# Two-layer hybrid encoder: matmuls grouped by shape, one pool of PSUM slots, three pieces of elementwise work on GpSimd

## The chip, the cores and the metric

The kernel runs on one core of a Trainium2 chip. The metric is device time in microseconds of one execution. Three executions of the kernel before took 1160.4, 1160.94 and 1161.4 us.

## The reference

The input x has 256 rows of 1024 features, mem 256 rows of 1024, all float32. Two layers are computed. Each has a token-mixing part and an MLP, each between two RMS norms, with the result added to x:

```python
h = rms_norm(x, norm_mix_pre[l])
zq, zk, zv, zx, zy, zxq, zg = in_projection(h, w_in[l])
q = apply_rope(zq.reshape(B, S, 8, 2, 64), cos, sin)
k = apply_rope(zk.reshape(B, S, 8, 2, 64), cos, sin)
y_attn = diff_attention(q, k, v, lam, diff_subln[l], lam_init)
xc = causal_conv(zx, conv_w[l], conv_b[l])
y_lru = rg_lru(xc, ...) * jax.nn.gelu(zy)
y_mem = memory_attention(zxq, mem, norm_mem[l], w_kv_mem[l])
gates = jax.nn.sigmoid(zg.reshape(B, S, 3, D_MODEL) + b_gate[l])
merged = gates[:, :, 0] * (y_attn @ w_proj_attn[l]) + gates[:, :, 1] * (y_lru @ w_proj_lru[l]) + gates[:, :, 2] * (y_mem @ w_proj_mem[l])
x = x + rms_norm(merged @ w_out[l], norm_mix_post[l])
h = rms_norm(x, norm_mlp_pre[l])
a = jax.nn.relu(h @ w_mlp_up[l])
x = x + rms_norm((a * a) @ w_mlp_down[l], norm_mlp_post[l])
```

The rotation (`apply_rope`) takes each pair of halves t1, t2 to t1 c - t2 s and t2 c + t1 s. `rg_lru` is a linear recurrence over the 256 positions, h = a h + u, with a and u from sigmoid gates.

## The kernel before

**Weights and precision.** Every large product is made in two parts. A weight chunk of 1 MB (`raw`, three buffers, loaded by SP in the order of use) is split in two halves, and each half into a rounded part `wh` (ScalarE, line 179) and a rest `wl` (VectorE, line 181), five buffers of each. `weights` issues loads up to four chunks ahead and splits up to five halves ahead. Activations are pairs hi and lo as well.

**Two kinds of product.** `mm_feat` (lines 236 to 254) makes 256 output features by 256 tokens: two halves of 128 features, each with eight steps over the 1024 inputs. At a step one matmul takes `wh` with hi and lo side by side (512 columns) and one takes `wl` with hi alone (256 columns). ScalarE copies the lo part out of PSUM into the tile `z`, VectorE adds the hi part (lines 252, 253). There are 128 such chunks in the two layers: memory keys, x, y, q, k, memory q, three branch gates, three branch projections, and MLP up. `mm_tok` (lines 256 to 280) makes tokens by 512 outputs, with three matmuls of 512 columns per step: v, memory values, output projection `wo`, MLP down `dn`. Its result for both row halves (t = 0 and 1) lies in one PSUM tile; in the last chunk of an output half n = 1, `apart` orders all matmuls of t = 0 ahead of those of t = 1.

```python
for k in range(8):
    pe.matmul(o.rearrange("p (s n) -> p s n", s=2), wh[:, k, :], av[:, :, k, :], start=(k == 0), stop=False)
    state["mm"] = pe.matmul(o[:, 0:256], wl[:, k, :], av[:, 0, k, :], start=False, stop=(k == 7))
```

**PSUM.** Accumulators of both kinds (`acc`, two banks each) come from a pool of two slots, scores of the differential attention (`sc`, two banks) from a pool of one, all smaller tiles (`at`) from two of one bank.

**Order.** The code is written in the order of the products. Other work runs beside them as generators (`side`), one step at each `tick`, and a scheduler sets the order on each engine: memory attention beside x and y, the recurrence `lru` beside y, q, k and v, the differential attention `attn` beside the three branches (order: memory, recurrence, attention). Each branch chunk is a gate product followed by a projection; `th` is the gate, `mg` the sum of the branches (lines 855 to 859).

**Rotation.** `rotary` takes each chunk of q and k (four of each per layer) from `z`: one product of 512 elements with cos, two of 256 with sin, one sum of 512, all on VectorE (lines 641 to 644), with the scale of q inside them. `by_head` then moves q or k to a layout by head with eight DMAs on SP (line 654); weight loads stand behind them in SP's queue. The first scores of the attention (line 670) need them.

**Recurrence.** Late in `lru`, four products of 512 elements (line 623) make the input u, one scan of 2048 elements (line 626) runs the recurrence, and four steps make the output `ylr`, with casts on ScalarE (lines 230, 231, 631).

**After `wo` and `dn`.** `post_half` squares and sums each row half on ScalarE (line 367) and scales it on VectorE (371); `post_end` makes the norm and adds to x (lines 382 to 388). The tmp pool has nine slots of 512 elements for z, the rotation's partial results and others.

Of the kernel before, what the change touches and what calls it, by code (L numbers as in the profile page):

```python
# [9 lines left out]
F32 = mybir.dt.float32  # L10
# [3 lines left out]
ALU = mybir.AluOpType  # L14
# [54 lines left out]
def trunk(ctx, tc, x_in, xt_in, mem_in, memt_in, w_in, par_in, lamv_in, post_in, rope_in, out):  # L69
# [6 lines left out]
    p_pair = ctx.enter_context(tc.tile_pool(name="pair", bufs=6))  # L76
    p_tmp = ctx.enter_context(tc.tile_pool(name="tmp", bufs=9))
    p_sm = ctx.enter_context(tc.tile_pool(name="sm", bufs=4))
    ps_acc = ctx.enter_context(tc.tile_pool(name="psacc", bufs=2, space=bass.MemoryType.PSUM))
    ps_sc = ctx.enter_context(tc.tile_pool(name="pssc", bufs=1, space=bass.MemoryType.PSUM))  # L80
    ps_at = ctx.enter_context(tc.tile_pool(name="psat", bufs=2, space=bass.MemoryType.PSUM))

    def pair(name):
# [28 lines left out]
        return p_sm.tile([128, n], F32, tag="sm_" + name, name=name)  # L112

    def sc():
        return ps_sc.tile([128, 1024], F32, tag="sc", name="sc")

    def acc():

        return ps_acc.tile([128, 2, 512], F32, tag="acc", name="acc")

    def acc_tok():
        a = acc()
        return [a[:, t, :] for t in range(2)]

# [9 lines left out]
    nc.sync.dma_start(out=par_all, in_=par_in)  # L134
    par = par_all[:, 0:DEPTH * NVEC * 8].rearrange("p (l v k) -> p l v k", l=DEPTH, v=NVEC)
    subln = par_all[:, DEPTH * NVEC * 8:DEPTH * NVEC * 8 + DEPTH]
    rope = const.tile([128, 2, 256], F32, name="rope")
    lamv = tmp("lamv").rearrange("p (l c d) -> p l c d", l=DEPTH, c=4)
    xt = const.tile([128, 2, 1024], F32, name="xt")

# [92 lines left out]
            act.activation(out=hi, in_=src, func=AF.Copy, scale=scale)  # L233
            dve.scalar_tensor_tensor(lo, src, scale, hi.bitcast(F32), op0=ALU.mult, op1=ALU.subtract)

    def mm_feat(key, a):

        ps = acc()
        av = hl(a)
        for j in range(2):
            wh, wl = (f8(t) for t in weights(*key, j))
            o = ps[:, j, :]
            for k in range(8):
                pe.matmul(o.rearrange("p (s n) -> p s n", s=2), wh[:, k, :], av[:, :, k, :], start=(k == 0), stop=False)  # L247
                state["mm"] = pe.matmul(o[:, 0:256], wl[:, k, :], av[:, 0, k, :], start=False, stop=(k == 7))  # L248
            if j == 0:
                tick()  # L250
        z = tmp("z")
        act.copy(two(z), ps[:, :, 256:512])  # L252
        dve.tensor_tensor(two(z), two(z), ps[:, :, 0:256], op=ALU.add)  # L253
        return z

    def mm_tok(pss, key, a_of, first, last, apart=False):
# [96 lines left out]
    def two(ap):  # L353
        return ap.rearrange("p (i n) -> p i n", i=2)
# [222 lines left out]
    def lru(l, xc, rgw, g2, done):  # L577
        wv = rgw.rearrange("p (c n d) -> p c n d", c=2, n=8)
        xv = f8(xc)
        av, tv = duo("lru")  # L580
        for j in range(4):
            sl = slice(j * 512, (j + 1) * 512)
            ti, xs = tv[:, sl], xc[:, sl]

            def gate(c):
                ps = at()
                for i in range(2):
                    f = 2 * j + i
# [13 lines left out]
            act.activation(out=xs, in_=xs, func=AF.Exp, scale=-1.0)
            yield
        act.activation(out=xc, in_=xc, func=AF.Ln, bias=1.0)
        yield
        for j in range(4):
            sl = slice(j * 512, (j + 1) * 512)
            a, xs = av[:, sl], xc[:, sl]
            act.activation(out=xs, in_=xs, func=AF.Exp, scale=-1.0)
            e = tmp("lE")  # L610
            for i in range(2):
                f = 2 * j + i
                act.activation(out=f8(av)[:, f, :], in_=f8(xc)[:, f, :], func=AF.Exp, scale=ncsp[:, l, f:f + 1])
                act.activation(out=e[:, i * 256:(i + 1) * 256], in_=f8(xc)[:, f, :], func=AF.Tanh,
                               scale=csp[:, l, f:f + 1])
            act.activation(out=xs, in_=a, func=AF.Square)
            dve.scalar_tensor_tensor(xs, xs, 1.0, e, op0=ALU.add, op1=ALU.mult)
            yield
        act.activation(out=xc, in_=xc, func=AF.Sqrt, scale=0.25)
        yield  # L620
        for j in range(4):
            sl = slice(j * 512, (j + 1) * 512)
            dve.tensor_tensor(tv[:, sl], tv[:, sl], xc[:, sl], op=ALU.mult)
        dve.memset(f8(av)[:, :, 0:1], 0.0)
        yield
        dve.tensor_tensor_scan(xc, av, tv, 0.0, op0=ALU.mult, op1=ALU.add)
        yield
        ylr = done["y"] = pair("ylr")
        for j in range(4):
            sl = slice(j * 512, (j + 1) * 512)  # L630
            dve.scalar_tensor_tensor(xc[:, sl], xc[:, sl], 0.5, g2[:, sl], op0=ALU.mult, op1=ALU.mult)
            split_to(hi(ylr)[:, sl], lo(ylr)[:, sl], xc[:, sl])
            yield


    def rotary(scale, j, ps, r):

        z = two(ps)
        cs, sn = rope[:, 0, :], rope[:, 1, :]
        m1, m2 = tmp("rp1"), tmp("rp2")  # L640
        dve.scalar_tensor_tensor(two(m1), z, scale, rows2(cs), op0=ALU.mult, op1=ALU.mult)
        dve.scalar_tensor_tensor(m2[:, 0:256], ps[:, 256:512], -scale, sn, op0=ALU.mult, op1=ALU.mult)
        dve.scalar_tensor_tensor(m2[:, 256:512], ps[:, 0:256], scale, sn, op0=ALU.mult, op1=ALU.mult)
        dve.tensor_tensor(r.rearrange("p (i j n) -> p i j n", i=2, j=4)[:, :, j, :], two(m1), two(m2), op=ALU.add)

    def by_head(r, dst):

# [9 lines left out]
    def attn(l, qT, kT, va, done):  # L657
# [3 lines left out]

        def scores(h):
            pbs[h] = []
            ps = sc().rearrange("p (c n) -> p c n", c=2)
            for b in range(2):
                nk = 128 * (b + 1)
                sv = ps[:, :, 128 * b:128 * b + nk]
# [98 lines left out]

    mem_keys(0, start_rows)
    nc.sync.dma_start(out=lamv, in_=lamv_in.partition_broadcast(128))
    nc.sync.dma_start(out=rope, in_=rope_in)
    load_rows(xt, x_in)  # L770
    xf, xj = duo("xf")
    nc.sync.dma_start(out=xf, in_=xt_in)
# [17 lines left out]
    for l in range(DEPTH):  # L790
# [31 lines left out]
        rq, rk = duo("rqk")  # L822
        for nm, scale, dst, r in (("q", 0.125, qT, rq), ("k", 1.0, kT, rk)):
            for j in range(4):
                ps = mm_feat((l, nm, j), hx)
                rotary(scale, j, ps, r)
                tick()
            by_head(r, dst)
        for n in range(2):
# [8 lines left out]
        for b, pj, yb in ((2, "pm", {"y": ym}), (1, "pl", ylr), (0, "pa", ya)):  # L838
# [4 lines left out]
            for j in range(4):  # L843
# [173 lines left out]
```

## Time and profile before

| | |
|---|---|
| median of three executions | 1160.94 us |
| the profiled execution | 1162.9 us |
| its span | 1161.1 us |
| TensorE busy | 1122.5 us, 97% |
| weight loads of TensorE | 956.6 us, 82% |
| VectorE busy | 863.4 us, 74% |
| ScalarE busy | 705.2 us, 61% |
| GpSimd busy | 0.7 us, six instructions |
| granted TensorE clock | 0.989 of full, mean |

Matmuls are pipelined, and their durations overlap in the trace: the pace of a stream is read from the starts, and a gap shows only where the engine was quite idle. The columns "idle before" give the time in which an engine stood before an instruction, and which instruction released it. The page's share of a whole span is a mean over stages with different limits, so what a stage waits for is read from its own rows.

### The profile page before, as it was taken

Reading aid. Unit: us, or ns where it says so; the run is one execution under the profiler, and the core shown is the slowest. Engines: PE = TensorE matmul, PEld = TensorE weight load, DVE = VectorE, ACT = ScalarE, POOL = GpSimd, SP = SyncE. Lnnn points to the kernel's source line nnn. Section 1 sums busy time; section 2 is a strip of 40 time slices with the busy share of each in tenths; the row PEclk is TensorE's granted clock in tenths of the full one; section 3 lists DMA queues with packets and bytes.
Section 4 is the critical chain, followed back from the end, with each engine's and each line's share of the span. In section 5 each row is a group of like instructions: output and inputs, shape, how many; then the busy total and the mean of one; then the engine's idle time right before and its main releaser. Section 6 shows DMA issues by size and latency. Waiting matters only on the chain. (4 is left out here: it accounts for less than half of the span.)

```text
span 1161.1 us, 15842 instructions
## 1 busy us (share of the span) xinstructions
PE 1122.5 (97%) x6096; PEld 956.6 (82%) x6096; DVE 863.4 (74%) x1347; ACT 705.2 (61%) x1112; POOL 0.7 (0%) x6
## 2 busy tenths in 40 slices
PE   7999999999999999999999999998999997999996
PEld 5789888778888888888888888877788886888885
DVE  6979789778877687774457787987888666887453
ACT  6756695656556566663446667947665554766341
POOL 0000000000000000000000000000000000000000
PEclk9999999989999999999999999999999998999998
DMA  9655346644456545555554534665344553556550
GB/s 326 242 215 181 110 155 207 217 145 146 145 204 214 192 173 185 187 183 205 201 202 167 210 109 145 213 213 179 122 146 167 212 183 109 187 199 213 181 181 37
DMA packets 34779, 209.28 MB, mean 180 GB/s; under 512 B 3856, under 2 KB 8080, under 8 KB 10768
## 3 DMA queue, kind: packets, MB, share of 16 engines
q1 hardware_dynamic: 34128, 206.18, 50.5%
q10 hardware_dynamic: 576, 2.10, 0.5%
q8 instruction: 48, 0.79, 0.3%
q14 instruction: 27, 0.22, 0.1%
HBM read 203.02 MB, written 1.05 MB: 176 GB/s over the span
## 5 line engine op out<-in xcount | busy, mean ns | idle before, releaser
L181 DVE TENSOR_TENSOR wl<-raw,wh 128x1024 fp32r<-128x1024 f32 (+1 forms) x369 | 449.1, 1220 | 216.1 <-ACT wh L179 215.0
L179 ACT CAST wh<-raw 128x1024 fp32r<-128x1024 f32 (+1 forms) x369 | 385.0, 1048 | 325.8 <-PE acc L247 166.5
L247 PE MATMUL acc<-hx,wh 128*128 128x512 f32 x1536 | 550.3, 401 | 6.5 <-ACT vmg L835 2.9
L248 PE MATMUL acc<-hx,wl 128*128 128x256 f32 x1536 | 432.9, 282 | 0.0
L247 PEld LDWEIGHTS acc<-hx,wh 128*128 128x128 f32 x1536 | 290.1, 189 | 77.4 <-ACT vmg L835 3.7
L248 PEld LDWEIGHTS acc<-hx,wl 128*128 128x128 f32 x1536 | 292.0, 190 | 2.5 <-issue 2.0
L266 PE MATMUL acc<-wh,sq 128*128 128x512 f32 x256 | 99.6, 389 | 0.0
L265 PE MATMUL acc<-wl,sq 128*128 128x512 f32 x256 | 99.6, 389 | 0.0
L264 PE MATMUL acc<-wh,sq 128*128 128x512 f32 x256 | 99.6, 389 | 0.0
L253 DVE TENSOR_TENSOR z<-z,acc 128x512 f32<-128x512 f32 x128 | 87.1, 681 | 8.7 <-ACT z L252 8.7
L252 ACT COPY z<-acc 128x512 f32<-128x512 f32 x128 | 74.3, 580 | 9.5 <-PE acc L248 9.4
L265 PEld LDWEIGHTS acc<-wl,sq 128*128 128x128 f32 x256 | 48.1, 188 | 10.0
L264 PEld LDWEIGHTS acc<-wh,sq 128*128 128x128 f32 x256 | 48.1, 188 | 10.0
L266 PEld LDWEIGHTS acc<-wh,sq 128*128 128x128 f32 x256 | 48.1, 188 | 9.9
L247 PE MATMUL acc<-mh,wh 128*128 128x512 f32 x128 | 47.7, 412 | 6.9 <-ACT wh L179 6.9
L247 PE MATMUL acc<-xq,wh 128*128 128x512 f32 x128 | 46.5, 401 | 1.1 <-ACT wh L179 1.1
L247 PE MATMUL acc<-ylr,wh 128*128 128x512 f32 x128 | 46.0, 401 | 0.5 <-DVE z L253 0.5
L247 PE MATMUL acc<-ya,wh 128*128 128x512 f32 x128 | 45.6, 399 | 0.0
L248 PE MATMUL acc<-mh,wl 128*128 128x256 f32 x128 | 36.9, 288 | 1.2 <-DVE wl L181 1.2
L248 PE MATMUL acc<-xq,wl 128*128 128x256 f32 x128 | 36.5, 285 | 1.5 <-DVE wl L181 1.5
L248 PE MATMUL acc<-ya,wl 128*128 128x256 f32 x128 | 36.0, 281 | 0.0
L248 PE MATMUL acc<-ylr,wl 128*128 128x256 f32 x128 | 35.8, 280 | 0.0
(202 smaller groups left out, 1407.2 us busy)
## 6 DMA issues: line engine op xcount, KB each, us to landing
raw<-in_w SPq DMA_DIRECT2D x183, 1024.0 KB, 4.8
qkT<-rqk SPq DMA_DIRECT2D x32, 128.0 KB, 4.4
rgw<-in_w SPq DMA_DIRECT2D x2, 1024.0 KB, 7.0
post<-in_post ACTq DMA_DIRECT2D x4, 512.0 KB, 4.1
mem<-in_memt SPq DMA_DIRECT2D x4, 256.0 KB, 4.6
memr<-in_mem SPq DMA_DIRECT2D x2, 512.0 KB, 7.1
xt<-in_x SPq DMA_DIRECT2D x2, 512.0 KB, 10.2
xf<-in_xt SPq DMA_DIRECT2D x1, 1024.0 KB, 12.1
```

The source lines that it names most:

```text
L179: act.copy(h[:, sl], r[:, sl])
L181: dve.tensor_tensor(l[:, sl], r[:, sl], h[:, sl].bitcast(F32), op=ALU.subtract)
L247: pe.matmul(o.rearrange("p (s n) -> p s n", s=2), wh[:, k, :], av[:, :, k, :], start=(k == 0), stop=False)
L248: state["mm"] = pe.matmul(o[:, 0:256], wl[:, k, :], av[:, 0, k, :], start=False, stop=(k == 7))
L252: act.copy(two(z), ps[:, :, 256:512])
L253: dve.tensor_tensor(two(z), two(z), ps[:, :, 0:256], op=ALU.add)
L264: pe.matmul(pss[t], ah[:, sl], wh[:, k, :], start=(first and half == 0 and k == 0), stop=False)
L265: pe.matmul(pss[t], ah[:, sl], wl[:, k, :], start=False, stop=False)
L266: m = pe.matmul(pss[t], al[:, sl], wh[:, k, :], start=False, stop=(last and half == 1 and k == 1))
```

## The change

1. `mm_feat` issues the eight `wh` matmuls of a half first, then the eight `wl` matmuls. Its evacuation gets high priority in the scheduler, and it can take a scale, which q uses (0.125).
2. `sc` is taken from the accumulators' pool, which now has three slots; the pool of scores is gone.
3. `rotary` runs on GpSimd. The scale is in z already; a third table, -sin, is made once.
4. The recurrence's four products go to GpSimd; its scan is cut into four of 512 elements.
5. The sum of the branch of the recurrence (b = 1) into `mg` goes to GpSimd.
6. For the output half n = 1 of `wo` and `dn`, each row half has an accumulator slot of its own.

```diff
-    ps_acc = ctx.enter_context(tc.tile_pool(name="psacc", bufs=2, space=bass.MemoryType.PSUM))
-    ps_sc = ctx.enter_context(tc.tile_pool(name="pssc", bufs=1, space=bass.MemoryType.PSUM))
+    ps_acc = ctx.enter_context(tc.tile_pool(name="psacc", bufs=3, space=bass.MemoryType.PSUM))
...
     def sc():
-        return ps_sc.tile([128, 1024], F32, tag="sc", name="sc")
+        return ps_acc.tile([128, 2, 512], F32, tag="acc", name="sc")
...
-    def acc_tok():
+    def acc_tok(apart=False):
+        if apart:
+            return [acc()[:, 0, :] for t in range(2)]
         a = acc()
         return [a[:, t, :] for t in range(2)]
...
             for k in range(8):
                 pe.matmul(o.rearrange("p (s n) -> p s n", s=2), wh[:, k, :], av[:, :, k, :], start=(k == 0), stop=False)
+            for k in range(8):
                 state["mm"] = pe.matmul(o[:, 0:256], wl[:, k, :], av[:, 0, k, :], start=False, stop=(k == 7))
...
         z = tmp("z")
-        act.copy(two(z), ps[:, :, 256:512])
-        dve.tensor_tensor(two(z), two(z), ps[:, :, 0:256], op=ALU.add)
+        with tc.high_priority():
+            if scale is None:
+                act.copy(two(z), ps[:, :, 256:512])
+                dve.tensor_tensor(two(z), two(z), ps[:, :, 0:256], op=ALU.add)
+            else:
+                act.activation(out=two(z), in_=ps[:, :, 256:512], func=AF.Copy, scale=scale)
+                dve.scalar_tensor_tensor(two(z), ps[:, :, 0:256], scale, two(z), op0=ALU.mult, op1=ALU.add)
...
-            dve.tensor_tensor(tv[:, sl], tv[:, sl], xc[:, sl], op=ALU.mult)
+            pool.tensor_tensor(tv[:, sl], tv[:, sl], xc[:, sl], op=ALU.mult)
         dve.memset(f8(av)[:, :, 0:1], 0.0)
         yield
-        dve.tensor_tensor_scan(xc, av, tv, 0.0, op0=ALU.mult, op1=ALU.add)
-        yield
+        for j in range(4):
+            sl = slice(j * 512, (j + 1) * 512)
+            dve.tensor_tensor_scan(xc[:, sl], av[:, sl], tv[:, sl], 0.0, op0=ALU.mult, op1=ALU.add)
+            if j % 2:
+                yield
...
-    def rotary(scale, j, ps, r):
+    def rotary(j, ps, r):
...
-        dve.scalar_tensor_tensor(two(m1), z, scale, rows2(cs), op0=ALU.mult, op1=ALU.mult)
-        dve.scalar_tensor_tensor(m2[:, 0:256], ps[:, 256:512], -scale, sn, op0=ALU.mult, op1=ALU.mult)
-        dve.scalar_tensor_tensor(m2[:, 256:512], ps[:, 0:256], scale, sn, op0=ALU.mult, op1=ALU.mult)
-        dve.tensor_tensor(r.rearrange("p (i j n) -> p i j n", i=2, j=4)[:, :, j, :], two(m1), two(m2), op=ALU.add)
+        pool.tensor_tensor(two(m1), z, rows2(cs), op=ALU.mult)
+        pool.tensor_tensor(m2[:, 0:256], ps[:, 256:512], ns, op=ALU.mult)
+        pool.tensor_tensor(m2[:, 256:512], ps[:, 0:256], sn, op=ALU.mult)
+        pool.tensor_tensor(r.rearrange("p (i j n) -> p i j n", i=2, j=4)[:, :, j, :], two(m1), two(m2), op=ALU.add)
...
-                    dve.tensor_tensor(mg[:, sl], mg[:, sl], th, op=ALU.add)
+                    (pool if b == 1 else dve).tensor_tensor(mg[:, sl], mg[:, sl], th, op=ALU.add)
...
-            pss = acc_tok()
+            pss = acc_tok(n == 1)
```

What the edits do to the order is seen at three places of layer 0. The first is TensorE at the step from v (`acc` fed by `wh` and `hx`, line 266, now 273) to the first branch gate and the first scores (line 670, now 680). Before:

```order
L266 MATMUL acc_2013<-wh_1992,hx_431 128x512
L247 MATMUL acc_2090<-hx_431,wh_2016 128x512 [waits Activation_49]
L248 MATMUL acc_2090<-hx_431,wl_2017 128x256 [waits DVE_49]
L247 MATMUL acc_2090<-hx_431,wh_2016 128x512
L248 MATMUL acc_2090<-hx_431,wl_2017 128x256
...
L670 MATMUL sc_2113<-qkT_1460 128x128 [waits DMAHW5_49,DMAHW6_49,DMAHW1_49,DMAHW0_49]
```

After:

```order
L273 MATMUL acc_2011<-wh_1989,hx_429 128x512
L248 MATMUL acc_2088<-hx_429,wh_2014 128x512 [waits PE_49,Activation_49]
L248 MATMUL acc_2088<-hx_429,wh_2014 128x512 x7
L250 MATMUL acc_2088<-hx_429,wl_2015 128x256 [waits DVE_49]
L250 MATMUL acc_2088<-hx_429,wl_2015 128x256 x7
L680 MATMUL sc_2111<-qkT_1458 128x128 [waits DMAHW4_49,DMAHW5_49,DMAHW1_49,DMAHW0_49]
```

The pairs have become two groups, and the wait for `wl` stands behind eight matmuls instead of one. The scores stand where they stood, behind half a gate chunk, and wait for the DMAs of q and k as before.

The second place is VectorE while the first three k chunks are evacuated (L181 and L182 are the weight splits, L253 and L260 the evacuation, `lru` the operands of the recurrence). Before:

```order
L253 TENSOR_TENSOR z<-z,acc 128x512 [waits Activation_49]
L623 TENSOR_TENSOR lru<-lru,xcg 128x512
L641 SCALAR_TENSOR_TENSOR rp_1863<-z,rope 128x512 [waits DVE_49]
L642 SCALAR_TENSOR_TENSOR rp_1864<-z,rope 128x256
L643 SCALAR_TENSOR_TENSOR rp_1864<-z,rope 128x256
L623 TENSOR_TENSOR lru<-lru,xcg 128x512
L644 TENSOR_TENSOR rqk<-rp_1863,rp_1864 128x2x256 [waits DVE_49]
L181 TENSOR_TENSOR wl<-raw,wh 128x1024 [waits DMAHW4_49,Activation_49]
L181 TENSOR_TENSOR wl<-raw,wh 128x1024 [waits PE_49,Activation_49]
L253 TENSOR_TENSOR z<-z,acc 128x512 [waits Activation_49]
L626 SCALAR_TENSOR_TENSOR xcg<-lru 128x2048 [waits DVE_49]
```

After:

```order
L182 TENSOR_TENSOR wl<-raw,wh 128x1024 [waits DMAHW3_49,PE_49,Activation_49]
L260 SCALAR_TENSOR_TENSOR z<-acc,z 128x512 [waits DVE_49,Activation_49]
L635 SCALAR_TENSOR_TENSOR xcg<-lru 128x512 [waits DVE_49,Pool_49]
L182 TENSOR_TENSOR wl<-raw,wh 128x1024 [waits PE_49,Activation_49]
L260 SCALAR_TENSOR_TENSOR z<-acc,z 128x512 [waits Activation_49]
L635 SCALAR_TENSOR_TENSOR xcg<-lru 128x512 [waits Pool_49] x3
L641 SCALAR_TENSOR_TENSOR xcg<-xcg 128x512 [waits DVE_49] x3
L232 TENSOR_TENSOR ylr<-xcg,ylr 128x512 [waits Activation_49] x3
L182 TENSOR_TENSOR wl<-raw,wh 128x1024 [waits DMAHW4_49,Activation_49]
L260 SCALAR_TENSOR_TENSOR z<-acc,z 128x512 [waits Activation_49]
```

The rotation and the products are gone from this queue. The scans now wait for GpSimd, and weight splits and evacuations stand behind those waits.

The third place is GpSimd's own queue at the same time, which held nothing before (`rp` are the rotation's partial results, `rqk` its output):

```order
L654 TENSOR_TENSOR rqk<-rp_1748,rp_1749 128x2x256 [waits Pool_49]
L630 TENSOR_TENSOR lru<-lru,xcg 128x512 [waits Activation_49]
L630 TENSOR_TENSOR lru<-lru,xcg 128x512 x2
L651 TENSOR_TENSOR rp_1808<-z,rope 128x512 [waits DVE_49]
L652 TENSOR_TENSOR rp_1809<-z,rope 128x256
L653 TENSOR_TENSOR rp_1809<-z,rope 128x256
L630 TENSOR_TENSOR lru<-lru,xcg 128x512
L654 TENSOR_TENSOR rqk<-rp_1808,rp_1809 128x2x256 [waits Pool_49]
L651 TENSOR_TENSOR rp_1861<-z,rope 128x512 [waits DVE_49]
```

The products of the recurrence stand between the rotations of the first and the second k chunk, so a late rotation holds up a scan, and a late product a rotation.

## Rows read from the trace of the kernel before

**Rows 1.** The page, part 1: busy time, share of the span, instructions.
```profile
PE 1122.5 (97%) x6096; PEld 956.6 (82%) x6096; DVE 863.4 (74%) x1347; ACT 705.2 (61%) x1112; POOL 0.7 (0%) x6
```
**Rows 2.** Busy time by stage: length; engines' busy us; granted clock; DMA share; GB/s.
```profile
180.00:210.00 30.00, 30.00 (x148) 25.04 (x147) 29.99 (x39) 16.25 (x18) 0.00 (x0) 1.00 0.65 189
```
**Rows 3.** Timeline of TensorE: start, us, line, output from input, shape, count.
```profile
83.79 1.60 PE L507 MATMUL at<-ka,xq 128*128 128x256 f32 x12
85.23 0.40 PE L247 MATMUL acc<-hx,wh 128*128 128x512 f32 x1
...
909.66 0.40 PE L247 MATMUL acc<-hx,wh 128*128 128x512 f32 x1
...
917.08 0.40 PE L247 MATMUL acc<-ya,wh 128*128 128x512 f32 x1
...
1000.27 0.39 PE L247 MATMUL acc<-hx,wh 128*128 128x512 f32 x1
...
1009.29 0.39 PE L247 MATMUL acc<-hx,wh 128*128 128x512 f32 x1
...
1145.82 0.39 PE L266 MATMUL acc<-wh,sq 128*128 128x512 f32 x1
...
1151.26 0.39 PE L266 MATMUL acc<-wh,sq 128*128 128x512 f32 x1
```
**Rows 4.** Timeline of TensorE at its waits; in brackets idle us and who ended them.
```profile
214.22 0.50 PE L247 MATMUL acc<-hx,wh 128*128 128x512 f32 x1 [1.43 <-ACT vmg L835]
...
221.71 0.49 PE L247 MATMUL acc<-xq,wh 128*128 128x512 f32 x1 [0.53 <-ACT wh L179]
...
222.97 0.39 PE L248 MATMUL acc<-xq,wl 128*128 128x256 f32 x1 [0.77 <-DVE wl L181]
...
234.94 0.93 PE L670 MATMUL sc<-qkT 64*128 64x128 f32 x8
...
244.78 0.93 PE L670 MATMUL sc<-qkT 64*128 64x128 f32 x8 [1.99 <-ACT ae L680]
...
246.33 0.77 PE L247 MATMUL acc<-hx,wh 128*128 128x512 f32 x1 [0.62 <-DVE z L253]
...
293.98 0.50 PE L247 MATMUL acc<-hx,wh 128*128 128x512 f32 x1 [0.68 <-DVE z L253]
...
781.75 0.50 PE L247 MATMUL acc<-hx,wh 128*128 128x512 f32 x1 [1.43 <-ACT vmg L835]
```
**Rows 5.** Timeline of ScalarE after v: the four copies of v's accumulators.
```profile
213.10 2.06 ACT L835 COPY vmg<-acc 128x512 f32<-128x512 f32 x4 [0.76 <-DVE ylr L231]
```
**Rows 6.** Busy time by stage, behind the 1.99 us wait.
```profile
246.00:252.00 6.00, 5.67 (x18) 4.93 (x19) 2.56 (x9) 2.10 (x7) 0.00 (x0) 0.50 0.01 5
```
**Rows 7.** Groups of VectorE: shapes, count, busy us, mean ns, idle before, releaser.
```profile
L181 DVE TENSOR_TENSOR wl<-raw,wh 128x1024 fp32r<-128x1024 f32 x367 | 447.8, 1223 | 215.3 <-ACT wh L179 214.3
...
L644 DVE TENSOR_TENSOR rqk<-rp,rp 128x512 f32<-128x512 f32 x16 | 11.0, 685 | 0.0
L641 DVE SCALAR_TENSOR_TENSOR rp<-z,rope 128x512 f32<-128x512 f32 x16 | 10.9, 684 | 0.1
...
L642 DVE SCALAR_TENSOR_TENSOR rp<-z,rope 128x256 f32<-128x256 f32 x16 | 6.7, 419 | 0.0
```
**Rows 8.** Timeline: first rotation of q, transfers of k on SP, first scores.
```profile
155.70 0.69 DVE L641 SCALAR_TENSOR_TENSOR rp<-z,rope 128x512 f32<-128x512 f32 x1
...
202.42 5.12 SPq L654 DMA_DIRECT2D qkT<-rqk  x8
...
217.24 0.93 PE L670 MATMUL sc<-qkT 64*128 64x128 f32 x8
```
**Rows 9.** Timeline behind layer 1's output projection, and at the kernel's end.
```profile
967.68 0.69 PE L318 MATMUL at<-ident,xt 128*128 128x128 f32 x2 [3.92 <-DVE xt L388]
...
1151.69 0.60 ACT L367 ACTIVATE junk<-acc 128x512 f32<-128x512 f32 x1 [12.54 <-PE acc L266]
...
1156.63 1.42 DVE L388 SCALAR_TENSOR_TENSOR xt<-post,ry,xt 128x512 f32<-128x512 f32 x2
```

More of the change, by code (lines that the diff above doesn't have):

```diff
@@ L234, in split_to, with mm_feat @@
             dve.scalar_tensor_tensor(lo, src, scale, hi.bitcast(F32), op0=ALU.mult, op1=ALU.subtract)
-    def mm_feat(key, a):
+    def mm_feat(key, a, scale=None):
         ps = acc()
@@ L633, in lru @@
             yield
-    def rotary(scale, j, ps, r):
+    def rotary(j, ps, r):
         z = two(ps)
-        cs, sn = rope[:, 0, :], rope[:, 1, :]
+        cs, sn, ns = (rope[:, i, :] for i in range(3))
         m1, m2 = tmp("rp1"), tmp("rp2")
-        dve.scalar_tensor_tensor(two(m1), z, scale, rows2(cs), op0=ALU.mult, op1=ALU.mult)
-        dve.scalar_tensor_tensor(m2[:, 0:256], ps[:, 256:512], -scale, sn, op0=ALU.mult, op1=ALU.mult)
-        dve.scalar_tensor_tensor(m2[:, 256:512], ps[:, 0:256], scale, sn, op0=ALU.mult, op1=ALU.mult)
-        dve.tensor_tensor(r.rearrange("p (i j n) -> p i j n", i=2, j=4)[:, :, j, :], two(m1), two(m2), op=ALU.add)
+        pool.tensor_tensor(two(m1), z, rows2(cs), op=ALU.mult)
+        pool.tensor_tensor(m2[:, 0:256], ps[:, 256:512], ns, op=ALU.mult)
+        pool.tensor_tensor(m2[:, 256:512], ps[:, 0:256], sn, op=ALU.mult)
+        pool.tensor_tensor(r.rearrange("p (i j n) -> p i j n", i=2, j=4)[:, :, j, :], two(m1), two(m2), op=ALU.add)
     def by_head(r, dst):
@@ L663, in scores @@
             pbs[h] = []
-            ps = sc().rearrange("p (c n) -> p c n", c=2)
+            ps = sc()
             for b in range(2):
@@ L768, in trunk @@
     nc.sync.dma_start(out=lamv, in_=lamv_in.partition_broadcast(128))
-    nc.sync.dma_start(out=rope, in_=rope_in)
+    nc.sync.dma_start(out=rope[:, 0:2, :], in_=rope_in)
+    pool.tensor_scalar(rope[:, 2, :], rope[:, 1, :], -1.0, None, op0=ALU.mult)
     load_rows(xt, x_in)
@@ L824, in trunk @@
             for j in range(4):
-                ps = mm_feat((l, nm, j), hx)
-                rotary(scale, j, ps, r)
+                ps = mm_feat((l, nm, j), hx, scale)
+                rotary(j, ps, r)
                 tick()
@@ L908, in trunk @@
         for n in range(2):
-            pss = acc_tok()
+            pss = acc_tok(n == 1)
             for c in range(8):
```

2 lines of the change are left out of this document (1 added, 1 removed).

## The prediction

> **What bounds the kernel now.** I read the page's busy times first: TensorE is busy for 1122.5 of 1161.1 us [rows 1], and the chain of waits runs mostly through its matmuls. So only two things count: how fast a stream of matmuls runs, and the gaps in it. The profiled execution took 1162.9 us, its span 1161.1; the median of the runs shown is 1160.94, 2.0 lower. I sum against 1162.9 and take the 2.0 off at the end. A measurement of this kernel can tell about 0.2% (2.3 us) from no change.
>
> Second, the timeline of TensorE, for the pace [rows 3]. A feature-major product alternates a 512-column matmul (wh) with a 256-column one (wl). It has two paces: from 909.66 to 917.08 lie 21 pairs of 353.3 ns, from 1000.27 to 1009.29 lie 26 of 346.9. Same instructions, same granted clock; the pace changes only after an interruption. Going through such first and last starts chunk by chunk, I count 78 of 128 chunks at the slow pace, some 1240 of 2048 pairs. Chains of one shape stand beside this: twelve 256-column matmuls, each with its own weights, take 1.44 us (83.79 to 85.23), 120 ns each; 24 of 512 columns take 5.44 us (1145.82 to 1151.26), 226.7 ns each.
>
> Third, TensorE's idle times [rows 4]. Two places in each layer carry them: the step from v to the first gate, and the attention scores that are mixed into the gate branches. Layer 1 repeats layer 0, of which 781.75 stands as an example.
>
> **The change part by part**, in us.
>
> *Grouping by shape.* A half of eight pairs becomes eight 512s, then eight 256s. By the pure chains that is 8 x (226.7 + 120) = 2774 ns, 346.7 per pair: the fast pace, to 0.2 ns. If all halves run so, 1240 pairs gain 6.6 ns: -8.2. At the other end, the slow pace belongs to the 512 itself and stays (353.3 less the 116.7 that a 256 takes between 512s), while each 256 now costs 120: 3.3 ns more on 1240 pairs, +4.1. I take **-5.0**, nearer the first end since both pure chains run at its sum. All wh of a half are now needed before its first wl, so wl may be some 1.8 late (8 x 226.7) at no cost; and where the moving operand arrives piece by piece (first chunk, and first chunk of layer 1's MLP) the eight 256s no longer fill the gaps: 8 x 0.12 = +1.0 there, which at the kernel's start the relaxed wl pays for.
>
> *Third shared slot, v to gate.* TensorE stood 1.43 because both accumulators of v waited for ScalarE [rows 4], which made all four copies at 213.10, behind the recurrence's casts and VectorE [rows 5]. With three slots the gate's accumulator is the one that k left: -1.43 in two layers, **-2.9**. At 221.71 and 222.97 it stood 0.53 and 0.77 for weight splits that were stuck behind the same copies; in the new order the copies stand earlier and four casts go ahead of the softmax: **-2.6** in two layers. If the third slot only moved the wait to these casts, this second term would be nothing.
>
> *Third slot, scores.* In layer 0 TensorE stood 1.99 for the one score slot, and 0.62 and 0.68 for accumulators [rows 4]: 3.3, and about as much in layer 1. The gain is between 6.6 and less than nothing, for the accumulator two products later now takes the slot that a softmax holds. I take half, **-3.3**. After the 1.99 gap the granted clock was 0.50 for 6 us [rows 6], the lower of its two levels: 3 us of work lost, in layer 0 alone. Half of that, **-1.5**.
>
> *Priority for the evacuation* of an accumulator costs no instruction; the splits that it passes are five halves ahead of TensorE (5 x 2.8 = 14 us), so nothing.
>
> *Rotary, product and sum to GpSimd.* VectorE loses 16 x (0.684 + 2 x 0.419 + 0.685) = 35 us in the two q/k stages [rows 7] and some 11 elsewhere. That earns nothing by itself: VectorE was full at 180 to 210 [rows 2] while TensorE had no gap there. What it costs hangs on GpSimd, of which the trace shows no such operation. Count in units of one 512-element operation: a rotation is three units (two whole, two halves), the four products of the recurrence four, 28 in all per layer, in GpSimd's own order, products between the rotations of k. They have from the first rotation, 155.7, to when the last k rotation must go to SP: the scores ran at 217.24, 215.8 without the 1.43 stall, and the eight transfers took 5.1 [rows 8], so 210.7. That is 55.0 us, **1.96 a unit**. VectorE takes 0.69. Up to 1.96 (2.9 times VectorE) the cover is the rest of q/k and the whole of v; beyond that each 0.1 costs 2.8 per layer, because TensorE waits for the transfers and the weight loads that stand behind them on SP [rows 8]. A gain is excluded, since VectorE's time is covered as it is; I take **+2.0** for operations that hold each other up, since no row shows two of them side by side. The Trainium skill (GPSIMD Engine Reference, sections 3.1 and 4.1) advises VectorE for such arithmetic and gives 4497 ns for an addition of 2048 elements: an estimate of 1.12 a unit, no run here shows it; with it 28 units are 31 of the 55 us, and the sum would stay as it is. The sum on the branch gate (one unit per chunk) is needed four products later and costs nothing unless GpSimd falls behind a whole branch.
>
> *Separate slots for the two row halves* of the last column half (output projection, MLP down). The last 12 matmuls then write only the second half, and the first half's chain starts 12 x 0.2267 = 2.7 earlier. That chain begins at 1151.69 and holds up the second, whose last addition is at 1156.63 [rows 9]; in the new order the second starts when the first has ended, so **-2.6** at the end of the kernel. The same shift in front of layer 1's MLP, where TensorE stood 3.92 [rows 9], less the 1.0 of grouping there, and some of it lost to the casts between: **-1.0**. In layer 0 other products cover both places: nothing.
>
> Sum: -5.0 -2.9 -2.6 -3.3 -1.5 -2.6 -1.0 +2.0 = -16.9. 1162.9 - 16.9 = 1146.0 for a profiled execution, less 2.0: **1144 us**. With each gain at its end and GpSimd free it is about 1131; with +4.1 for grouping and nothing at the scores about 1158.
>
> **The rivals.**
>
> *A slot swapped for a wait (the change frees no wait).* Scores that needed one slot now keep accumulators waiting; one softmax held its slot from 234.94 to 244.78 [rows 4], longer than the seven us or so (a product and a score) that now lie between a score and the second product after it. Then the 3.3, the 1.5 and half of the casts' 2.6 do not come: 1144 + 6 = 1150. For it: the softmax is as long as before. Against: VectorE enters this stage less laden.
>
> *VectorE and GpSimd in each other's way.* Per chunk of q/k VectorE has two splits of 1.22 and one recurrence step of 0.69, 3.1 [rows 7], and a chunk lasts 5.6; three units on GpSimd at twice VectorE are 4.1. Side by side that fits; one after the other it makes 7.2, 1.6 too long, 13 over eight chunks, and the splits lead by 14 at most. I put 5 per layer on TensorE: 1154. The row for it is that VectorE was full here; against it, that 17 us of rotary leave it. The Trainium skill (SBUF — State Buffer, section on SBUF's two separate sides) has such a rule: GpSimd and a VectorE operation with two SBUF inputs lock each other out for a whole instruction; no run here shows it, and by it the time would be this rival's.
>
> *GpSimd too slow: slower than before.* One mechanism: the last k rotation reaches SP after 210.7, and scores and weight loads wait. It decides from 1.96 a unit. At 2.45 (3.6 times VectorE) it is 28 x 0.49 = 13.7 per layer, 27 in all; without the 2.0 above, 1142 + 27 = 1169. Nothing in the trace bounds a unit from above, which is why it keeps a chance.
>
> **How the numbers follow.** Forecast 0.62; slot swapped 0.13; in each other's way 0.13; GpSimd too slow 0.12. The range runs from the low end of the forecast, with a little for waits hidden in overlapped matmuls, to beyond 1154 and the forecast's own worst sum: 1129 to 1161. Outside lie the slow case and some of the low side. Faster by over 0.2%: all but the slow case and a small part of the two middle ones, 0.83; within 0.2%: 0.04; slower: 0.13.
>
> **What would show it.** Grouping: TensorE's starts within one half at 226 to 230 ns, then at 120; halves of 2.77 us in all stages. Slots: no idle of 1.4 after v, no wait of a score for ScalarE, granted clock 1.0 through the scores. GpSimd: a rotation of 3 to 5 us, the last transfers of k leaving SP by 205, VectorE under nine tenths busy at 180 to 210. End: the first square about 2.7 before the last matmul's. The prediction is wrong if a unit on GpSimd takes over 1.96, if VectorE's splits grow beside it, or if halves take 2.83 as before.

## The result and the profile after

The changed kernel takes 1167.43 us (median of four, 1165.1 to 1167.9) beside 1161.14 of the kernel before in the same runs: a ratio of 1.0051, with a 95% interval of 1.0034 to 1.0069. It is slower, by some 6 us, where 17 less was forecast. The profiled execution took 1167.43 us, its span 1165.6. The page's busy times, answering to [rows 1], and the shares of its chain of waits:

```profile
PE 1119.0 (96%) x6096; PEld 961.6 (82%) x6096; DVE 866.0 (74%) x1273; ACT 705.0 (60%) x1112; POOL 130.6 (11%) x87
...
PE 76%; issue 11%; POOL 7%; DVE 3%; ACT 2%; DMA 1%; SPq 0%; DVEq 0%; POOLq 0%
```

GpSimd, which is busy for 11% of the span, makes 7% of the chain. And VectorE is as busy as before (863.4) with 74 fewer instructions. Both are explained below. The busy time by stage shows where TensorE stops; the first row stands beside [rows 2], where TensorE was busy for all 30 us:

```profile
180.00:210.00 30.00, 17.84 (x81) 14.33 (x81) 23.72 (x18) 9.13 (x12) 26.27 (x19) 0.81 0.45 143
...
204.00:212.00 8.00, 6.01 (x13) 4.42 (x14) 8.00 (x9) 5.26 (x8) 4.59 (x3) 0.50 0.29 98
```

TensorE's timeline at its waits, beside [rows 4] (idle time and releaser in brackets; layer 1 repeats it at 774.73 and 777.15 with 10.56 and 1.62):

```profile
204.36 0.80 PE L271 MATMUL acc<-wh,hx 128*128 128x512 f32 x1 [10.54 <-ACT wh L180]
206.78 0.79 PE L272 MATMUL acc<-wl,hx 128*128 128x512 f32 x1 [1.63 <-DVE wl L182]
...
208.23 0.63 PE L272 MATMUL acc<-wl,hx 128*128 128x512 f32 x1
208.65 0.63 PE L273 MATMUL acc<-wh,hx 128*128 128x512 f32 x1
...
253.39 0.93 PE L680 MATMUL sc<-qkT 64*128 64x128 f32 x8 [1.64 <-ACT ae L690]
```

The 1.43 after v is gone, as is every wait for an accumulator between the gates. In their place stands one wait of 10.5 us inside v for a weight cast, and 1.6 for the split behind it. After such a pause the granted clock is 0.50, the lower of the two levels, until about 212: matmuls of 512 columns then start 0.43 apart.

Why a weight cast was late is read from the other engines' timeline of the same stretch:

```profile
182.40 0.74 POOL L652 TENSOR_TENSOR rp<-z,rope 128x256 f32<-128x256 f32 x1
...
183.91 1.28 POOL L654 TENSOR_TENSOR rqk<-rp,rp 128x512 f32<-128x512 f32 x1
185.16 4.71 POOL L630 TENSOR_TENSOR lru<-lru,xcg 128x512 f32<-128x512 f32 x3
186.48 2.30 DVE L635 TENSOR_TENSOR_SCAN xcg<-lru 128x512 f32<-128x512 f32 x1 [4.28 <-POOL lru L630]
...
188.70 2.25 DVE L182 TENSOR_TENSOR wl<-raw,wh 128x1024 fp32r<-128x1024 f32 x1
189.83 2.28 POOL L651 TENSOR_TENSOR rp<-z,rope 128x512 f32<-128x512 f32 x1
190.87 0.68 DVE L260 SCALAR_TENSOR_TENSOR z<-acc,z 128x512 f32<-128x512 f32 x1
...
195.28 1.26 POOL L630 TENSOR_TENSOR lru<-lru,xcg 128x512 f32<-128x512 f32 x1
...
196.57 2.27 DVE L635 TENSOR_TENSOR_SCAN xcg<-lru 128x512 f32<-128x512 f32 x1 [1.77 <-POOL lru L630]
...
200.56 0.62 ACT L231 CAST ylr<-xcg 128x512 fp32r<-128x512 f32 x1 [17.09 <-DVE xcg L641]
...
203.26 1.04 ACT L180 CAST wh<-raw 128x1024 fp32r<-128x1024 f32 x1
...
205.51 1.21 DVE L182 TENSOR_TENSOR wl<-raw,wh 128x1024 fp32r<-128x1024 f32 x1
...
214.67 5.12 SPq L664 DMA_DIRECT2D qkT<-rqk  x8
```

It is read from the bottom upward. TensorE waits for the cast at 203.26. That cast stands in ScalarE's queue behind the cast of `ylr`, which waited 17.09 us for VectorE; VectorE's step 641 stands behind the four scans. These wait for GpSimd's products (4.28 and 1.77 us), of which the last stands behind a rotation's first three operations. That is a chain through four engines' queues. Its links are also slow. In these rows an operation of 512 elements takes GpSimd 1.26 to 1.28 us where VectorE stands idle, and 2.28 beside VectorE's work; a weight split takes VectorE 2.25 instead of 1.22 [rows 7]. GpSimd's groups over the whole kernel (mean in ns) give a rotation of 2003 + 1354 + 1431 + 1808 ns = 6.6 us, where a chunk takes TensorE 5.6:

```profile
L651 POOL TENSOR_TENSOR rp<-z,rope 128x512 f32<-128x512 f32 x16 | 32.1, 2003 | 508.9 <-DVE z L260 508.9
L654 POOL TENSOR_TENSOR rqk<-rp,rp 128x512 f32<-128x512 f32 x16 | 28.9, 1808 | 1.1
L653 POOL TENSOR_TENSOR rp<-z,rope 128x256 f32<-128x256 f32 x16 | 22.9, 1431 | 0.0
L652 POOL TENSOR_TENSOR rp<-z,rope 128x256 f32<-128x256 f32 x16 | 21.7, 1354 | 0.0
```

### The profile page after: what moved, and what is told of

Its sections match the earlier page's. It is cut to its first block, busy times and chain, and to the rows that moved or that the text cites. A ratio compares the mean times of both kernels' runs of the same rounds, so it can differ in the third digit from the quotient of the medians.

```text
span 1165.6 us, 15911 instructions
## 1 busy us (share of the span) xinstructions
PE 1119.0 (96%) x6096; PEld 961.6 (82%) x6096; DVE 866.0 (74%) x1273; ACT 705.0 (60%) x1112; POOL 130.6 (11%) x87
## 4 chain that ended last, share of the span: by engine, by line
PE 76%; issue 11%; POOL 7%; DVE 3%; ACT 2%; DMA 1%; SPq 0%; DVEq 0%; POOLq 0%
PE acc L248 31%; PE acc L250 16%; PE acc L272 8%; PE acc L273 8%; PE acc L271 8%; POOL rp L651 2%; POOL rqk L654 2%; POOL rp L653 1%; POOL rp L652 1%; PE sc L680 1%; POOL lru L630 1%; PE at L715 1%; DMA rope<-in_rope 1%; DVE xcg L641 1%; PE at L596 1%
## 5 line engine op out<-in xcount | busy, mean ns | idle before, releaser
L182 DVE TENSOR_TENSOR wl<-raw,wh 128x1024 fp32r<-128x1024 f32 (+1 forms) x369 | 467.7, 1273 | 195.9 <-ACT wh L180 194.3
L248 PE MATMUL acc<-hx,wh 128*128 128x512 f32 x1536 | 393.3, 397 | 1.3 <-DVE hx L235 1.3
L250 PEld LDWEIGHTS acc<-hx,wl 128*128 128x128 f32 x1536 | 209.7, 190 | 15.8 <-issue 0.7
L250 PE MATMUL acc<-hx,wl 128*128 128x256 f32 x1536 | 214.8, 282 | 0.0
L651 POOL TENSOR_TENSOR rp<-z,rope 128x512 f32<-128x512 f32 x16 | 32.1, 2003 | 508.9 <-DVE z L260 508.9
L271 PE MATMUL acc<-wh,hx 128*128 128x512 f32 x64 | 27.4, 429 | 21.1 <-ACT wh L180 21.1
L870 POOL TENSOR_TENSOR vmg<-vmg,th 128x512 f32<-128x512 f32 x8 | 12.9, 1613 | 236.0 <-DVE th L869 116.8
L248 PEld LDWEIGHTS acc<-mh,wh 128*128 128x128 f32 x128 | 24.3, 198 | 12.9 <-ACT wh L180 6.8
L271 PEld LDWEIGHTS acc<-wh,hx 128*128 128x128 f32 x64 | 13.4, 209 | 24.8 <-ACT wh L180 21.9
L248 PE MATMUL acc<-ylr,wh 128*128 128x512 f32 x128 | 32.6, 396 | 0.0
```

Of the source, the lines that this page charges most:

```text
L182: dve.tensor_tensor(l[:, sl], r[:, sl], h[:, sl].bitcast(F32), op=ALU.subtract)
L271: pe.matmul(pss[t], ah[:, sl], wh[:, k, :], start=(first and half == 0 and k == 0), stop=False)
L651: pool.tensor_tensor(two(m1), z, rows2(cs), op=ALU.mult)
L870: (pool if b == 1 else dve).tensor_tensor(mg[:, sl], mg[:, sl], th, op=ALU.add)
```

## The experiments

Two theories stood against each other: that the result of GpSimd comes late and waits in other queues pass this on to TensorE (the chain above), or that GpSimd's work slows VectorE down, whoever waits for the result. In each diff the minus is the version named.

**1. The changed kernel with the rotation on VectorE.**

```diff
-        pool.tensor_tensor(two(m1), z, rows2(cs), op=ALU.mult)
+        dve.tensor_tensor(two(m1), z, rows2(cs), op=ALU.mult)
...
```

> The changed kernel with the rotation back on VectorE, all else as changed (the products of the recurrence and the branch sum stay on GpSimd). Theory A (the loss is a chain of queues: late rotations on GpSimd hold the recurrence's products, these hold VectorE's scans, these hold ScalarE's casts of ylr, and TensorE waits in v for the weight casts behind them): both waits of 10.5 and 1.6 us at the start of v and the half-clock stretch behind them go, some 14 us per layer; 1167 becomes 1137 to 1142. Theory B (the parts that were to gain bring nothing, the loss lies elsewhere): about 1160, as before the change.

It took 1147.38 us (0.9878 of the kernel before, interval 0.9861 to 0.9894), 20 less than the changed kernel. That is 5 above the upper end of theory A and 13 below theory B. TensorE's wait in v is

```profile
201.83 0.80 PE L272 MATMUL acc<-wl,hx 128*128 128x512 f32 x1 [2.14 <-DVE wl L182]
```

So most of the loss needs the rotation on GpSimd. What is left in v is a wait for VectorE's split; a wait of 2.11 for a weight cast at the first gate stands beside it.

**2. The changed kernel with the recurrence's products on VectorE**, the rotation on GpSimd.

```diff
-            pool.tensor_tensor(tv[:, sl], tv[:, sl], xc[:, sl], op=ALU.mult)
+            dve.tensor_tensor(tv[:, sl], tv[:, sl], xc[:, sl], op=ALU.mult)
```

> The changed kernel with the four products of the recurrence back on VectorE, rotation on GpSimd. Theory A: the scans no longer wait for GpSimd, so the wait at the start of v shrinks to 0 to 4 us per layer, though operations that exclude each other still slow both engines; 1141 to 1150. Theory C (it is the late rotation itself that costs, through the transfers of q and k, which the scores and the weight loads on SP wait for): the wait moves to the scores or to weight loads and stays at 8 us per layer or more; 1155 to 1167.

It took 1156.67 us (0.9958, 0.9943 to 0.9973). The number lies with theory C, but not by its mechanism: no score waits for a transfer. No scan waits for GpSimd any more either, and yet TensorE stands in v, now for a weight split of VectorE, which is busy for 23.0 of the 23.0 us from 180 to 203. In the stretch from 150 to 240 that split has a mean of 1493 ns in place of 1218:

```profile
203.26 0.80 PE L272 MATMUL acc<-wl,hx 128*128 128x512 f32 x1 [7.88 <-DVE wl L182]
```
```profile
L182 DVE TENSOR_TENSOR wl<-raw,wh 128x1024 fp32r<-128x1024 f32 x29 | 42.9, 1493 | 1.8 <-ACT wh L180 1.8
```

The chain of queues alone (theory A as it stood) falls with that: without its first link two thirds of the wait remain.

**3 and 4. The kernel before with grouping alone, and with the three shared slots alone.**

```diff
             for k in range(8):
                 pe.matmul(o.rearrange("p (s n) -> p s n", s=2), wh[:, k, :], av[:, :, k, :], start=(k == 0), stop=False)
+            for k in range(8):
                 state["mm"] = pe.matmul(o[:, 0:256], wl[:, k, :], av[:, 0, k, :], start=False, stop=(k == 7))
```

> The kernel before with the grouping by shape alone. Slow and fast pace belong to the alternation (theory A): all halves at 2.77 us, 1240 of 2048 pairs gain 6.6 ns, 8 us: 1153. The slow pace belongs to the 512-column matmul (theory B): 1161 to 1165.

```diff
-    ps_acc = ctx.enter_context(tc.tile_pool(name="psacc", bufs=2, space=bass.MemoryType.PSUM))
-    ps_sc = ctx.enter_context(tc.tile_pool(name="pssc", bufs=1, space=bass.MemoryType.PSUM))
+    ps_acc = ctx.enter_context(tc.tile_pool(name="psacc", bufs=3, space=bass.MemoryType.PSUM))
```

> The kernel before with the three shared PSUM slots alone. If a third slot frees TensorE after v and at the scores (theory A): 2.9 for the copies of v, 2.6 for the casts behind them and some 3 at the scores: 1152. If the slot is only swapped for a wait at the scores (theory B): 2.9 at most, 1158 to 1161.

Grouping: 1155.80 us (0.9950, 0.9933 to 0.9967), 6.0 less than before, between the two theories and near the 5.0 of the prediction. Slots: 1154.73 us (0.9940, 0.9921 to 0.9959), 7.0 less; the interval, 4.8 to 9.2 less, does not reach the 10.3 that the prediction's four terms make. Both parts gain, so the loss lies elsewhere.

**5. Slots, and separate slots for the row halves** (the edits of the change to `acc_tok`, on top of 4).

> The kernel before with the three shared slots and the separate slots of the last column half, nothing else. If the prediction's terms for the separate slots hold (2.6 at the kernel's end, 1.0 in front of layer 1's MLP), it takes 1150 to 1152, 3 less than the shared slots alone (1154.7), and the first square of the last sum starts about 2.7 before the last matmul ends. If the casts and norms behind the last matmul take the time back, it stays at 1154 to 1155.

1151.30 us (0.9902, 0.9889 to 0.9916), 10.8 less than before, 3.7 more than in 4. The term holds. In the changed kernel's own timeline the first square now starts 2.7 before the second, and the last addition 2.65 after the last matmul's start, where [rows 3, 9] have 1156.63 - 1151.26 = 5.37:

```profile
1156.21 0.60 ACT L374 ACTIVATE junk<-acc 128x512 f32<-128x512 f32 x1 [9.82 <-PE acc L273]
...
1158.50 0.39 PE L273 MATMUL acc<-wh,sq 128*128 128x512 f32 x1
1158.93 0.60 ACT L374 ACTIVATE junk<-acc 128x512 f32<-128x512 f32 x1 [1.60 <-PE acc L273]
...
1161.15 1.41 DVE L395 SCALAR_TENSOR_TENSOR xt<-post,ry,xt 128x512 f32<-128x512 f32 x2
```

**6. The changed kernel with all three pieces of work on VectorE.**

```diff
-        pool.tensor_tensor(two(m1), z, rows2(cs), op=ALU.mult)
+        dve.tensor_tensor(two(m1), z, rows2(cs), op=ALU.mult)
...
-            pool.tensor_tensor(tv[:, sl], tv[:, sl], xc[:, sl], op=ALU.mult)
+            dve.tensor_tensor(tv[:, sl], tv[:, sl], xc[:, sl], op=ALU.mult)
...
-                    (pool if b == 1 else dve).tensor_tensor(mg[:, sl], mg[:, sl], th, op=ALU.add)
+                    dve.tensor_tensor(mg[:, sl], mg[:, sl], th, op=ALU.add)
```

> The changed kernel with all three pieces of work back on VectorE: rotation, products of the recurrence, sum of the gated branch. Theory A (what GpSimd does costs time, and the rest of the change earns what was summed for it): 1142 to 1146, a little under the kernel with the rotation alone on VectorE (1147.4), since its waits of 2.1 us at v and at the gate, behind products that GpSimd makes late, go. Rival B (VectorE is then too full at 180 to 210, and work on GpSimd earns something once the rotation is off it): 1148 to 1152, with waits for VectorE's weight splits at v.

1142.78 us (0.9830, 0.9816 to 0.9843), as theory A had it. The wait in v is gone; one of 2.11 at the first gate and one of 1.64 at the scores are left per layer. So the wait at the gate, other than the expectation said, does not come from late products of GpSimd.

```profile
PE 1114.5 (98%) x6096; PEld 959.3 (84%) x6096; DVE 862.6 (76%) x1353; ACT 704.6 (62%) x1112; POOL 1.5 (0%) x7
...
212.10 2.11 PE L248 MATMUL acc<-hx,wh 128*128 128x512 f32 x8 [2.11 <-ACT wh L180]
```

This closes the account of the changed kernel. Its idle time in v is 2 x (10.54 + 1.63) = 24.3, less the 2 x 2.11 that this kernel has instead: 20.1. TensorE's busy time is 1119.0 against 1114.5, 4.5 more, in good part at the lower clock. Together 24.6; the spans differ by 1165.6 - 1141.1 = 24.5.

**7. Before, with grouping and both kinds of slots, nothing else.** No priority for the evacuation, one scan of 2048, nothing on GpSimd (the edits of 3 and 5 together).

> The kernel before with grouping, shared slots and separate slots, nothing on GpSimd, no priority for the evacuation and one scan of 2048. If the terms add up (5.9 and 7.0 measured alone, 3 for the separate slots), 1144 to 1147. Against the kernel with everything on VectorE it tells what the priority and the scan in four pieces do: nothing by the prediction (within 1.5 of it); if the priority matters, 3 or more apart.

1142.21 us (0.9826, 0.9812 to 0.9839), the fastest kernel of this study, as fast as the one of experiment 6 and 2 below what was expected: measured one by one the three parts gained 6.0, 7.0 and, on top of the slots, 3.7; together they gain 19.8, and no run tells why. Priority, scan and the scale of q, the differences to experiment 6, change together which waits of TensorE are left, hardly their sum: here 0.63, 1.07, 1.15 and 0.62 per layer, there 2.11 and 1.64.

**8. A shadow on GpSimd.** The kernel of experiment 7, whose rotation is VectorE's; beside it GpSimd makes products that nobody reads.

```diff
         m1, m2 = tmp("rp1"), tmp("rp2")
+        for a, b in ((0, cs), (1, cs), (1, sn), (0, sn), (0, cs), (1, sn)):
+            pool.tensor_tensor(shad, ps[:, a * 256:(a + 1) * 256], b, op=ALU.mult)
```

(The expectation speaks of the first of the six as taken from `z`; as run, all six are.)

> As the kernel with grouping, shared and separate slots, but beside each rotation on VectorE GpSimd makes six products of 256 elements into a scratch tile that nobody reads (the first of them from z, so that they run when a rotation would). Theory A (the two engines hold each other up, whoever waits for the result): 5 to 14 us more than without them, VectorE's weight splits grow from 1.23 to 1.5 us or more beside them, waits for splits appear at v. Rival B (a late result is what costs): the same time as without them, within 1.5 us.

1187.50 us (1.0216, 1.0202 to 1.0230): 45 us more than without the shadow, three times what theory A's upper end gave. VectorE's groups from 150 to 240, without the shadow (experiment 7):

```profile
L182 DVE TENSOR_TENSOR wl<-raw,wh 128x1024 fp32r<-128x1024 f32 x31 | 37.3, 1218 | 4.2 <-ACT wh L180 4.2
L255 DVE TENSOR_TENSOR z<-z,acc 128x512 f32<-128x512 f32 x10 | 6.8, 682 | 3.7 <-ACT z L254 3.6
L646 DVE TENSOR_TENSOR rqk<-rp,rp 128x512 f32<-128x512 f32 x8 | 5.5, 684 | 0.0
...
L645 DVE SCALAR_TENSOR_TENSOR rp<-z,rope 128x256 f32<-128x256 f32 x8 | 3.4, 419 | 0.0
```

and with it:

```profile
L183 DVE TENSOR_TENSOR wl<-raw,wh 128x1024 fp32r<-128x1024 f32 x20 | 28.9, 1454 | 0.0
L649 DVE TENSOR_TENSOR rqk<-rp,rp 128x512 f32<-128x512 f32 x8 | 9.8, 1220 | 0.0
...
L648 DVE SCALAR_TENSOR_TENSOR rp<-z,rope 128x256 f32<-128x256 f32 x8 | 7.6, 952 | 0.0
L256 DVE TENSOR_TENSOR z<-z,acc 128x512 f32<-128x512 f32 x8 | 5.4, 676 | 3.3 <-ACT z L255 3.3
```

An operation of 256 elements goes from 0.42 to 0.95, one of 512 from 0.68 to 1.22: both are 0.53 to 0.54 longer, whatever their own length, as if each waits for one operation of GpSimd. The addition of `z`, which takes one operand from PSUM, stays at 0.68. Over the kernel VectorE is busy for 909.6 us against 861.3; the 48.3 more are 0.50 for each of the 96 operations of GpSimd. The pages, without the shadow and with it:

```profile
PE 1114.5 (98%) x6096; PEld 958.5 (84%) x6096; DVE 861.3 (76%) x1347; ACT 706.4 (62%) x1112; POOL 0.7 (0%) x6
...
PE 1131.1 (95%) x6096; PEld 966.7 (82%) x6096; DVE 909.6 (77%) x1347; ACT 705.7 (60%) x1112; POOL 112.5 (9%) x102
```

TensorE's waits now stand in k and in v, for VectorE's splits, though nothing waits for GpSimd's result. The longest are 3.03, 3.46, 3.15 and 3.22 per layer. Two of them:

```profile
189.32 1.21 PE L251 MATMUL acc<-hx,wl 128*128 128x256 f32 x8 [3.03 <-DVE wl L183]
...
201.34 0.80 PE L268 MATMUL acc<-wl,hx 128*128 128x512 f32 x1 [3.46 <-DVE wl L183]
```

That rules out rival B, a late result as the only cost. The 45 us are not the price of this in the changed kernel, though: here VectorE keeps the rotation, and the shadow comes on top.

**9. The shadow with one operand.** Six scaled copies in place of six products.

```diff
-        for a, b in ((0, cs), (1, cs), (1, sn), (0, sn), (0, cs), (1, sn)):
-            pool.tensor_tensor(shad, ps[:, a * 256:(a + 1) * 256], b, op=ALU.mult)
+        for b in (ps[:, 0:256], cs, sn, sn, cs, sn):
+            pool.tensor_scalar(shad, b, 2.0, None, op0=ALU.mult)
```

> As the shadow before (work of GpSimd beside the rotation, read by nobody), but each of the six operations reads one tile (a scaled copy) in place of two. If what holds VectorE up is that GpSimd is at work at all, whatever its operands, VectorE's two-operand operations stay about twice as long (0.95 to 1.2 us for the rotation's) and the time is 1170 to 1190. If it takes two operands on GpSimd's side as well, VectorE's durations stay at 0.42, 0.68 and 1.22 and the time is that without the shadow, 1142.

1154.63 us (0.9939, 0.9921 to 0.9957): 12 more than without a shadow, between the two expectations. VectorE's rotation operations of 512 elements are 0.2 longer, not 0.54 (from 150 to 240 again):

```profile
L183 DVE TENSOR_TENSOR wl<-raw,wh 128x1024 fp32r<-128x1024 f32 x29 | 35.7, 1246 | 2.8 <-ACT wh L181 2.8
L649 DVE TENSOR_TENSOR rqk<-rp,rp 128x512 f32<-128x512 f32 x8 | 7.0, 878 | 0.0
```

GpSimd's own operations over the kernel, first in experiment 8, then here:

```profile
L645 POOL TENSOR_TENSOR shad<-z,rope 128x256 f32<-128x256 f32 x96 | 111.8, 1165 | 689.5 <-DVE z L256 682.7
...
L645 POOL TENSOR_SCALAR shad<-rope 128x256 f32<-128x256 f32 x80 | 107.9, 1349 | 6.6
L645 POOL TENSOR_SCALAR shad<-z 128x256 f32<-128x256 f32 x16 | 22.4, 1403 | 648.5 <-DVE z L256 647.4
```

**10. Experiment 7 with the sum of the recurrence's branch on GpSimd**, the change's fifth edit alone.

> The kernel with grouping, shared and separate slots (1142.2), and of the work on GpSimd only the sum of the branch of the recurrence: eight operations of 512 elements in all, each needed four products later, in a stage where VectorE is three quarters busy. By the prediction's term for it (nothing): 1141 to 1143.5. If the engines' holding each other up costs there too, 2 or more: 1144 to 1146, with later evacuations or softmax steps of VectorE in the stage of the second branch.

1142.63 us (0.9837, 0.9820 to 0.9855): no difference to experiment 7 that the intervals, some 2 us to either side, can tell, as the prediction had it. VectorE is busy for 861.9 us, where it was 861.3 with these eight operations on it: they cost it about what they save. From 285 to 335, where the first four run, VectorE has room (39.5 of 50 us busy), and TensorE has no gap.

## Why the prediction was wrong

**The step that failed** is the term "I take **+2.0** for operations that hold each other up". Against the kernel with that work on VectorE (experiment 6) it measures +24.6. It had been taken without a row that shows the two engines side by side. All other terms together were -18.9; experiment 7, which has these parts alone, measures 1142.21 - 1162.05 = -19.8. That near agreement is partly luck, as the terms below show. (The low end of the sum, given as about 1131, comes to 1134 by the ends given for its terms; nothing hangs on it.)

Two things went wrong in it. The size: GpSimd's own speed was not the trouble. Undisturbed, a rotation is 1.28 + 0.74 + 0.74 + 1.28 = 4.0 us, 1.3 a unit, well under the 1.96 that I had set as the limit. Beside VectorE it is 6.6, or 2.2 a unit, and VectorE loses as well: with that unit and the split of 2.25, two of the prediction's own signs of being wrong came true. (The estimate of 1.12 a unit from the Trainium skill, GPSIMD Engine Reference, section 3.1, is near the undisturbed 1.3 and far from the 2.2.) VectorE's account in the changed kernel: 35.3 us of rotations and 16 operations of 0.685 have left it, 46.3 in all, and yet its busy time is 866.0 against 862.6 in experiment 6. So it was held up for about 50 us. An estimate from the rows agrees: in the shadow an operation of GpSimd of 256 elements holds VectorE up for 0.53, and the split of 2.25 in place of 1.22 gives 1.03 for one of 512. The change moves 48 operations of 512 and 32 of 256, which could cost 66 us; some three quarters of that came. The prediction had VectorE's 17 us of rotation per layer leave it; they came back as waiting, in a stretch where [rows 2] show it full. The place: I had looked for the late result only at the transfers of q and k. The last of them did leave at 214.67, beyond the 210.7 that I had allowed, but TensorE had lost its 12 us in v before that, through VectorE and ScalarE, where the new wait of the scans stood ahead of weight splits and casts.

**The rivals.** "In each other's way" was the right mechanism, with a price of 5 per layer where 12 came: I had weighed only the splits' lead, and no chain behind the scans. "GpSimd too slow" gave 1169, near the result by luck: the unit became slow only beside VectorE, and no score waited for a transfer. The rule of the Trainium skill (SBUF — State Buffer, section on who interferes with whom) says that a VectorE instruction with two SBUF inputs contends with a GpSimd instruction that reads SBUF, and one with at most one SBUF input, outside VectorE's 2-port modes, does not. The trace agrees: in experiment 8 0.68 became 1.22 for the first kind, and 0.68 stayed 0.68 for `z` with its PSUM operand. The prediction had this rule and gave its rival 0.13.

**Grouping (-5.0): the size right, the pace not.** It gains 6.0 alone, and 9.1 between experiments 5 and 7. One half in the changed kernel takes 2.80, not the 2.774 of the sum:

```profile
456.87 2.00 PE L248 MATMUL acc<-hx,wh 128*128 128x512 f32 x8
458.71 1.11 PE L250 MATMUL acc<-hx,wl 128*128 128x256 f32 x8
459.67 2.00 PE L248 MATMUL acc<-hx,wh 128*128 128x512 f32 x8
```

That is 350 ns a pair, where the sum had 346.7. With the prediction's own count, the slow pairs gain 1240 x 3.3 ns and the fast ones lose 808 x 3.1, so the pace earns an estimated 1.6 us and no more. Another part is the clock: behind the scores, where the kernel before has 0.50 [rows 6], the profiled execution of experiment 3 has 1.00:

```profile
242.00:248.00 6.00, 4.21 (x29) 3.30 (x28) 4.37 (x12) 4.33 (x13) 0.00 (x0) 1.00 0.49 175
248.00:254.00 6.00, 6.00 (x40) 4.82 (x39) 5.51 (x12) 4.32 (x11) 0.00 (x0) 1.00 0.42 157
```

By the prediction's reading of [rows 6] that is worth 3 us; it had booked them under the slots. How the 6.0 and the 9.1 divide, no run shows.

**Third slot (-2.9, -2.6, -3.3, -1.5, together -10.3): the first right, the rest mixed.** Experiment 4 gives -7.0. The 1.43 after v is gone. The casts behind the copies stay (0.60 and 0.76 there), so that term was nothing; of the waits at the scores 1.99 and 0.63 stay and 0.68 goes. The low clock behind the scores did go there (granted 1.00 from 242 to 254); in experiment 7 some of it is back, 0.77 from 242 to 248. So the rival of a slot swapped for a wait was partly true.

**Separate slots (-2.6, -1.0): right.** The rows show 2.7 at the end; in front of layer 1's MLP the idle times are 0.29, 2.65, 1.31 and 0.69, 4.9 in all, where before they were 3.92 and, behind it, 1.41 and 0.65: 1.0 less.

**The sum on the gated branch (nothing): right**, by experiment 10.

What stays open: how the 24.6 divide between contention and chain in the changed kernel. Rotation and sum on GpSimd, without the products, cost 13.9 (experiment 2 against 6); products and sum, without the rotation, 4.6 (1 against 6); the 6 that are left come only with both, where products stand behind rotations, and no run separates them further.

## What to carry to other kernels

Before work goes from VectorE to GpSimd, count the two-input operations that stay on VectorE in that stretch: in experiment 8 nearly every GpSimd product held one of them up. A stretch in which VectorE is full was the worst place here, not the best. When an engine gets a new wait, list what stands behind that wait on its queue and follow it until TensorE; a deadline for the obvious consumer is not enough. And a shadow, work that nobody reads, shows contention apart from lateness in one run, though not its price where the work has really moved.

## What the hardware showed beyond that

GpSimd's products of two operands held the rotation's operations on VectorE up by 0.53 us (256 elements), whatever their length; its scaled copies of one operand held those of 512 elements up by only about 0.2, though these copies took GpSimd itself longer (mean 1.35 to 1.40 against 1.17 us). By the rule of the Trainium skill named above (SBUF — State Buffer, section on who interferes with whom) both read SBUF and should contend alike. The size of the hold differs here, and no run tells why: the copies differ from the products in the operation and in the tiles that they read as well.

Grouped, a pair costs 350 ns, between the two paces of 346.9 and 353.3 that alternating pairs showed: by the starts above, the 512-column matmul takes 1.84 / 8 = 0.230 us, not the 226.7 ns of a chain of its own kind. In the stretches read, grouped halves had this one pace, whereas the alternating order kept the pace that its last interruption left it.
